# A weight-split step given a higher scheduling priority in a hybrid diffusion trunk kernel

## The chip, the cores and the metric

The kernel runs on one core of a Trainium2 chip. The metric is the device time of one execution in microseconds (us). Each core has five engines that run their own instruction lists in order and wait for one another through semaphores: TensorE (PE, matrix products; its weight loads are listed as PEld), VectorE (DVE), ScalarE (ACT), GpSimd (POOL) and SyncE (SP, which here only issues transfers).

## The reference

One step of a two-layer trunk on 128 context tokens and 256 latent tokens, D_MODEL = 1024, all in float32. Layer 0 mixes with a Mamba-2 head group and an RWKV-7 head group, layer 1 with a gated-linear-attention (GLA) and an mLSTM head group; each layer ends in a squared-ReLU MLP. Cut to its core:

```python
def sandwich_block(x, mod, mix_fn, g, w_up, w_down):
    shift1, scale1, gate1, shift2, scale2, gate2 = jnp.split(mod, N_MOD, axis=-1)
    m, st = mix_fn(rmsnorm(x, g[0]) * (1 + scale1) + shift1)
    x = x + gate1 * rmsnorm(m, g[1])
    f = jnp.square(jax.nn.relu((rmsnorm(x, g[2]) * (1 + scale2) + shift2) @ w_up)) @ w_down
    return x + gate2 * rmsnorm(f, g[3]), st

# mix_fn, layer 0: proj = h @ w_in (1024 x 6560); conv + SSD scan || RWKV-7 scan; concat @ w_out
# mix_fn, layer 1: proj = h @ w_in (1024 x 6192); GLA scan || conv + mLSTM; concat @ w_out
def rwkv step(s, inp):          # one of the scans
    s_kk = einsum('bhvk,bhk->bhv', s, kk_t)
    s = s * exp(lw_t) - s_kk[..., None] * (kk_t * a_t) + v_t[..., None] * k_t
    return s, einsum('bhvk,bhk->bhv', s, r_t)
```

The outputs are the two token arrays and the final scan states of each mixer.

## The kernel before

All 384 tokens stand side by side as the free dimension of [128, 384] tiles. The large products (input and output projections, MLP) are **dense** products. Their float32 operands are split in a high part, rounded to the matmul type, and a low part, the remainder: w = wH + wL and x = xH + xL, and each product is three matmuls, wH*xH, wH*xL and wL*xH. The activations are split once per layer. The weights come as panels, most of them 128 rows x 2 blocks x 128 columns (a 128x256 tile), 8 blocks in the MLP.

The way of a panel is: a transfer into a tile `raw` (line 695, from the SP queue), then `panel_split` (line 706): a copy on ScalarE, `wH<-raw` (line 714 through the helper on line 277), and a subtraction on VectorE, `wL<-raw,wH` (line 715 through line 235; a few go to GpSimd), then six matmuls `dps<-hnH,wH`, `dps<-hnL,wH`, `dps<-hnH,wL` for two blocks (lines 746 to 749 through line 221). `Dense.take(i)` (line 152) calls the split for the panel that it hands out and for `ahead` later ones, so that in source order a panel is split `ahead` panels before its matmuls. The buffers are few: in layer 0's mixer (line 1962) 5 raw tiles, 4 pairs of wH and wL, ahead 3; in layer 1's mixer 6, 6 and 4; in the MLP 3, 2 and 1. A wH copy therefore also waits until TensorE has read the panel that had the same buffer.

In the mixers the dense products are the filler of a pipeline. `run` (line 1584) draws steps from several generators (three stages of the RWKV-7 chain, `chain`, `inv` and `prep`; the SSD core; the dense panels as `fill`) by the pace table on line 34, and so sets the source order. That order is only a priority: the framework's scheduler walks a model of the engines, and on each engine it takes, of the instructions that are ready, the one that stands first in the source. What it puts out is the fixed list that each engine then runs on the chip. Tile names that come up below: `Zb`, `T`, `W`, `AO`, `pz`, `pt`, `pw`, `pe`, `pc` belong to the inverse of a 64x64 triangular matrix per head (`inv`), `R`, `UV`, `S`, `KR`, `py`, `pu`, `pd`, `pf` to the state chain, `psc`, `Q`, `BK` to its scores, and `cacc` is the accumulator of the 3x3 convolution.

The stages of the span: 0 to 60 us loads and the first norms, 60 to 170 us the start of layer 0's projections, 170 to 880 us layer 0's mixer with its end, 880 to 1185 us its MLP, 1185 to 1600 us layer 1's mixer, 1600 to 1851 us its MLP.

Of the kernel before, what the change touches and what calls it, by code (L numbers as in the profile page):

```python
# [8 lines left out]
F32 = mybir.dt.float32  # L9
# [5 lines left out]
ALU = mybir.AluOpType  # L15
# [160 lines left out]
class Net:  # L176
# [529 lines left out]
    def panel_split(self, cfg, raw):  # L706
        _, nk, ncol = raw.shape
        h = cfg["pool"].tile([128, nk, ncol], F32R, tag="wH", name="wH", bufs=cfg["split"])
        lo = cfg["pool"].tile([128, nk, ncol], F32R, tag="wL", name="wL", bufs=cfg["split"])
        hk = 512 // ncol  # L710
        self.nsplit += 1
        eng = self.nc.gpsimd if self.lpool and self.nsplit % self.lpool == 0 else None
        for q in (slice(i, min(nk, i + hk)) for i in range(0, nk, hk)):
            self.acopy(h[:, q], raw[:, q])
            self.tt(lo[:, q], raw[:, q], h[:, q].bitcast(F32), ALU.subtract, eng=eng)
        return h, lo

    def dacc(self):
# [1861 lines left out]
```

## Time and profile before

| | |
|---|---|
| median of 3 runs | 1855.35 us (1853.92 to 1860.46) |
| the profiled execution | 1853.32 us, its span 1851.2 us, 2.1 us outside the span |
| TensorE busy | 95% of the span, 13661 matmul records |
| TensorE weight loads | 80% |
| VectorE, ScalarE, GpSimd busy | 70%, 58%, 12% |
| mean granted clock of TensorE | 0.98 |
| chain that ended last | PE 75%, DVE 10%, ACT 8%, DMA 4% |

A share of busy time is a mean over stages with different limits: by the 40 slices of the page TensorE is busy for 70 to 90% of the first three slices and over 90% in nearly all later ones, VectorE is busiest in the mixers. Matmul ends are modelled, so that two matmuls that overlap in the pipeline both count; the start times are what to go by. The idle time in front of an instruction and what ended it stand in square brackets in a timeline.

### The profile page before, as it was taken

To read this page: it belongs to the slowest core of one execution; us is meant where nothing else is said; L and a number is where in the kernel's file an instruction comes from. 1 tells how busy PE (TensorE), PEld (TensorE's weight loads), DVE (VectorE), ACT (ScalarE), POOL (GpSimd) and SP (SyncE) were. 2 spreads that over 40 slices of the span, in tenths; PEclk is the share of its full clock that TensorE was granted. 3 is DMA by queue.
4 is the path that set the end of the run, shared out by engine and by line. 5 is a ranking of instruction groups with operands and counts; after the bars stand their busy time and mean duration, and the time that the engine had idled before them with its cause. 6 is when DMAs were issued, how large, how long until landed. Compare 5 with 4: busy or idle time off the path is not lost.

```text
span 1851.2 us, 37384 instructions
## 1 busy us (share of the span) xinstructions
PE 1765.5 (95%) x13661; PEld 1480.9 (80%) x13661; DVE 1301.8 (70%) x2992; ACT 1069.6 (58%) x2688; POOL 216.6 (12%) x270
## 2 busy tenths in 40 slices
PE   7879999999999999999999999899999998999998
PEld 3667767766666677786999998889989897999887
DVE  3698788777878889758766334786786958766434
ACT  3567475746574777646655333777676756755322
POOL 3222111110112011101000000020211212000000
PEclk9889999999999999999999999999999998999999
DMA  8332443333334322345445643333333233344432
GB/s 280 112 88 65 123 133 97 106 87 112 102 105 126 101 65 81 100 119 175 117 124 171 177 146 101 102 91 102 102 94 92 74 108 106 115 125 126 150 134 80
DMA packets 314107, 213.55 MB, mean 115 GB/s; under 512 B 39648, under 2 KB 297494, under 8 KB 313924
## 3 DMA queue, kind: packets, MB, share of 16 engines
q1 hardware_dynamic: 308756, 208.35, 38.6%
q10 hardware_dynamic: 4816, 2.69, 0.5%
q8 instruction: 107, 1.75, 0.4%
q14 instruction: 76, 0.62, 0.1%
q0 software_dynamic: 352, 0.13, 0.0%
HBM read 201.32 MB, written 9.78 MB: 114 GB/s over the span
## 4 chain that ended last, share of the span: by engine, by line
PE 75%; DVE 10%; ACT 8%; DMA 4%; issue 2%; POOL 1%; SPq 0%; DVEq 0%; ACTq 0%; POOLq 0%
PE dps L221 45%; PE o L221 7%; PE ps L221 4%; PE mod L221 3%; PE aux L221 2%; DVE wL L235 2%; PE psc L221 2%; DMA raw<-in_w_mod 2%; PE py L221 1%; PE pt L221 1%; DVE cacc L242 1%; PE pr L221 1%; ACT wH L277 1%; PE pw L221 1%; ACT Zb L277 1%
## 5 line engine op out<-in xcount | busy, mean ns | idle before, releaser
L277 ACT ACTIVATE wH<-raw 128x256 fp32r<-128x256 f32 (+1 forms) x790 | 363.3, 480 | 429.3 <-PE dps L221 309.6
L235 DVE TENSOR_TENSOR wL<-raw,wH 128x256 fp32r<-128x256 f32 (+2 forms) x771 | 398.9, 536 | 243.2 <-ACT wH L277 239.5
L277 ACT ACTIVATE Zb<-pz 64x384 f16<-64x384 f32 x160 | 77.2, 483 | 36.4 <-PE pz L221 34.1
L242 DVE SCALAR_TENSOR_TENSOR cacc<-rows,params,cacc 128x384 f32<-128x384 f32 (+1 forms) x192 | 94.2, 491 | 0.7
L221 PE MATMUL dps<-sH,wH 128*128 128x384 f32 x232 | 85.8, 371 | 4.0 <-DVE m L235 3.5
L221 PE MATMUL dps<-sL,wH 128*128 128x384 f32 x232 | 80.5, 347 | 0.3 <-DVE sL L235 0.2
L221 PE MATMUL dps<-sH,wL 128*128 128x384 f32 x232 | 79.7, 345 | 0.5 <-DVE wL L235 0.5
L221 PE MATMUL dps<-h0H,wH 128*128 128x384 f32 (+1 forms) x147 | 58.9, 401 | 8.2 <-ACT h0H L277 3.5
L235 DVE TENSOR_TENSOR AO<-AHb,rwmask 128x768 f16<-128x768 f16 (+1 forms) x112 | 60.1, 537 | 7.7 <-PE pz L221 6.0
L235 POOL TENSOR_TENSOR BK<-BK,kkk 128x768 f32<-128x768 f32 x16 | 33.8, 2110 | 221.5 <-DVE BK L239 150.5
L221 PE MATMUL mod<-xT,cond 128*32 128x384 f32 (+1 forms) x320 | 55.2, 485 | 3.8 <-DVE Q L235 2.5
L221 PE MATMUL dps<-h6H,wH 128*128 128x384 f32 (+2 forms) x147 | 54.9, 373 | 2.7 <-ACT wH L277 2.7
L221 PE MATMUL dps<-h2H,wH 128*128 128x384 f32 (+1 forms) x147 | 55.6, 378 | 1.4 <-ACT wH L277 1.4
L221 PE MATMUL dps<-h4H,wH 128*128 128x384 f32 (+1 forms) x147 | 54.9, 378 | 2.1 <-ACT h4H L245 2.1
L235 POOL TENSOR_TENSOR gDb<-gb 128x384 f32<-128x384 f32 x28 | 33.2, 1187 | 173.5 <-DVE gb L2230 73.2
L221 PE MATMUL dps<-h1H,wH 128*128 128x384 f32 (+1 forms) x147 | 52.0, 354 | 0.0
L221 PE MATMUL dps<-h6H,wL 128*128 128x384 f32 (+2 forms) x147 | 50.8, 346 | 1.2 <-DVE wL L235 1.2
L221 PE MATMUL dps<-h0H,wL 128*128 128x384 f32 (+1 forms) x147 | 51.7, 351 | 0.0
L221 PE MATMUL dps<-h1H,wL 128*128 128x384 f32 (+1 forms) x147 | 51.6, 351 | 0.0
L221 PE MATMUL dps<-h0L,wH 128*128 128x384 f32 (+1 forms) x147 | 51.5, 356 | 0.0
L221 PE MATMUL dps<-h1L,wH 128*128 128x384 f32 (+1 forms) x147 | 51.3, 355 | 0.0
L221 PE MATMUL dps<-h2H,wL 128*128 128x384 f32 (+1 forms) x147 | 51.1, 348 | 0.0
(1163 smaller groups left out, 5450.0 us busy)
## 6 DMA issues: line engine op xcount, KB each, us to landing
raw<-in_w_mlp_up SPq DMA_DIRECT2D x64, 512.0 KB
raw<-in_w_mlp_down SPq DMA_DIRECT2D x64, 512.0 KB
raw<-in_w_in_ab SPq DMA_DIRECT2D x204, 128.0 KB
xT<-in_w_mod SPq DMA_DIRECT2D x128, 192.0 KB
raw<-in_w_in_cd SPq DMA_DIRECT2D x192, 128.0 KB
raw<-in_w_mod SPq DMA_DIRECT2D x64, 192.0 KB
raw<-in_w_mod SPq DMA_DIRECT2D x32, 256.0 KB
raw<-in_w_out_cd SPq DMA_DIRECT2D x64, 128.0 KB
```

Of the source, the lines that this page charges most:

```text
L221: self.nc.tensor.matmul(out, lhsT, rhs, start=start, stop=stop)
L235: return (eng or self.nc.vector).tensor_tensor(out=out, in0=a, in1=b, op=op)
L242: self.nc.vector.scalar_tensor_tensor(out=out, in0=a, scalar=s, in1=b, op0=op0, op1=op1)
L277: self.nc.scalar.activation(out=out, in_=in_, func=AF.Copy)
```

## The change

The copy and the subtraction of `panel_split` are put in a block that lowers their priority number by 200, so that the scheduler ranks them as if they stood 200 instructions further up in the source. What they read, write and wait for stays as it is; no other priority changes. The number of instructions that compute is the same on every engine (2687 activations, 2992 on VectorE, 11552 matmul instructions); only their order moves.

```diff
         eng = self.nc.gpsimd if self.lpool and self.nsplit % self.lpool == 0 else None
-        for q in (slice(i, min(nk, i + hk)) for i in range(0, nk, hk)):
-            self.acopy(h[:, q], raw[:, q])
-            self.tt(lo[:, q], raw[:, q], h[:, q].bitcast(F32), ALU.subtract, eng=eng)
+
+        with self.tc.high_priority(offset=200):
+            for q in (slice(i, min(nk, i + hk)) for i in range(0, nk, hk)):
+                self.acopy(h[:, q], raw[:, q])
+                self.tt(lo[:, q], raw[:, q], h[:, q].bitcast(F32), ALU.subtract, eng=eng)
         return h, lo
```

Set side by side by instruction, the two orders differ so. Of the 176 subtractions on VectorE that ran between 170 and 800 us before, 133 now stand ahead of at least one instruction that they stood behind, 1342 such passings in all; of the 182 copies on ScalarE in that stretch it is 85, with 484 passings. Between 1185 and 1500 us it is 102 of 202 and 67 of 198; in the two MLPs (880 to 1185 and 1600 to 1851 us) 20 of 260 on VectorE. On TensorE the dense matmuls stand further ahead of the other matmuls in some places, by up to 22 near 275 to 330 us, 24 near 650 us, 16 near 790 us and 25 near 1480 us, and at the end of each such stretch the two orders meet again.

One place in layer 0's mixer, 284 to 297 us of the trace before, shows it on three engines. First VectorE, before: the subtractions of the panels 4231, 4267 and 4306 (the numbers tell the tiles apart).

```order
L235 TENSOR_TENSOR Q_4136<-psc_4168,rwmask_758 128x384
L235 TENSOR_TENSOR wL_4185<-raw_4182,wH_4184 128x256
L1382 COPY S_4210<-S0_2223 128x64
L1196 SCALAR_TENSOR_TENSOR b_4226<-r64_759,xT6_3651 128x384
L235 TENSOR_TENSOR R_4213<-pr_4212,R0_3523 128x64
L235 TENSOR_TENSOR wL_4231<-raw_4228,wH_4230 128x256
L235 TENSOR_TENSOR wL_4267<-raw_4264,wH_4266 128x256
L235 TENSOR_TENSOR xT6_3651<-b_4226,xT6_3651 128x384
L239 TENSOR_SCALAR UV_2678<-pu_4257 64x2x64
L235 TENSOR_TENSOR wL_4306<-raw_4303,wH_4305 128x256
```

And VectorE now: the same three subtractions, with the convolution taps (`cacc`) and, one row below this piece, `T_4047<-T_3975,pt2_4034`.

```order
L235 TENSOR_TENSOR wL_4231<-raw_4228,wH_4230 128x256
L242 SCALAR_TENSOR_TENSOR cacc_3929<-rows0_725,params_79,cacc_3929 128x384
L239 TENSOR_SCALAR UV_2678<-pu_4003 64x64
L242 SCALAR_TENSOR_TENSOR cacc_3929<-rows0_725,params_79,cacc_3929 128x384
L235 TENSOR_TENSOR wL_4267<-raw_4264,wH_4266 128x256
L242 SCALAR_TENSOR_TENSOR cacc_3929<-rows0_725,params_79,cacc_3929 128x192
L235 TENSOR_TENSOR modsb_3601<-modsb_3601,mod_4013 128x384
L242 SCALAR_TENSOR_TENSOR cacc_3929<-rows0_725,params_79,cacc_3929 128x192
L235 TENSOR_TENSOR W_4048<-W_3976,pw2_4027 128x384
L242 SCALAR_TENSOR_TENSOR cacc_3929<-rows0_725,params_79,cacc_3929 128x192
L235 TENSOR_TENSOR wL_4306<-raw_4303,wH_4305 128x256
L242 SCALAR_TENSOR_TENSOR cacc_3929<-rows0_725,params_79,cacc_3929 128x192
```

Before, `T_4047` stood 25 rows and more ahead of these subtractions; now all three stand ahead of it.

ScalarE at the same place, before: the copies `wH`, the chain's `Zb` and `UV`, the convolution's activation `Y`.

```order
L277 ACTIVATE wH_4230<-raw_4228 128x256
L277 ACTIVATE Zb_797<-pz_3994 64x6x64 x2
L245 ACTIVATE UV_2678<-pu_4003 64x64
L277 ACTIVATE wH_4266<-raw_4264 128x256
L277 ACTIVATE wH_4305<-raw_4303 128x256
L277 ACTIVATE Zb_797<-pz_4068 64x6x64 x2
L245 ACTIVATE Y_4008<-cacc_3929 128x384
L245 ACTIVATE Y_4008<-Y_4008 128x384 x2
L277 ACTIVATE W_4134<-pt_4119 128x384
L277 ACTIVATE xt_4280<-aux_4277 128x256
L245 ACTIVATE UV_2678<-pu_4147 64x64
```

ScalarE now: the copy of panel 4380, which stood behind `Z_4341<-dps_4181` further down, and the evacuation `Z_4341` of the dense column 4181 have come in front of `Zb_797<-pz_4068`.

```order
L277 ACTIVATE wH_4230<-raw_4228 128x256
L277 ACTIVATE Zb_797<-pz_3994 64x6x64 x2
L277 ACTIVATE wH_4266<-raw_4264 128x256
L245 ACTIVATE UV_2678<-pu_4003 64x64
L277 ACTIVATE wH_4305<-raw_4303 128x256
L277 ACTIVATE wH_4380<-raw_4378 128x256
L277 ACTIVATE Z_4341<-dps_4181 128x384
L245 ACTIVATE sg_4343<-Z_4341 128x384
L245 ACTIVATE sg_4343<-sg_4343 128x384
L277 ACTIVATE Zb_797<-pz_4068 64x6x64 x2
L245 ACTIVATE Y_4008<-cacc_3929 128x384
L277 ACTIVATE wH_4413<-raw_4411 128x256
```

`Zb_797<-pz_4068` now stands behind one more copy, an evacuation and two activations.

TensorE at the same place, before: the dense column `dps_4181` breaks off behind the second matmul of panel 4184, and the chain's `pz_4068` follows.

```order
L221 MATMUL dps_4181<-h5H_610,wH_3898 128x384
L221 MATMUL dps_4181<-h5L_611,wH_3898 128x384
L221 MATMUL dps_4181<-h5H_610,wL_3899 128x384
L232 MATMUL aux_4277<-const_base_77,X_3874 128x128
L221 MATMUL dps_4181<-h6H_619,wH_4184 128x384
L221 MATMUL dps_4181<-h6L_620,wH_4184 128x384
L221 LDWEIGHTS AO0_793
L221 MATMUL pz_4068<-T_4047,AO0_793 128x64
```

TensorE now: the column `dps_4181` is finished and the next one, `dps_4377`, begun ahead of `pz_4068`.

```order
L221 MATMUL dps_4181<-h6H_619,wH_4184 128x384
L221 MATMUL dps_4181<-h6L_620,wH_4184 128x384
L221 MATMUL dps_4181<-h6H_619,wL_4185 128x384
L221 MATMUL dps_4181<-h7H_628,wH_4184 128x384
L221 MATMUL dps_4181<-h7L_629,wH_4184 128x384
L221 MATMUL dps_4181<-h7H_628,wL_4185 128x384
L221 MATMUL dps_4377<-h0H_392,wH_4230 128x384
L221 MATMUL dps_4377<-h0L_393,wH_4230 128x384
L221 LDWEIGHTS AO0_793
L221 MATMUL pz_4068<-T_4047,AO0_793 128x64
```

Six dense matmuls have come in front of `pz_4068` here, and more stand between the chain's matmuls that follow.

## Rows read from the trace of the kernel before

**Rows 1.** The page, part 1: busy us, share of the span, instructions.

```profile
PE 1765.5 (95%) x13661; PEld 1480.9 (80%) x13661; DVE 1301.8 (70%) x2992; ACT 1069.6 (58%) x2688; POOL 216.6 (12%) x270
```

**Rows 2.** Stretches: length; PE, PEld, DVE, ACT, POOL busy us (count); clock, DMA share, GB/s.

```profile
60.00:170.00 110.00, 95.40 (x725) 78.40 (x724) 89.92 (x212) 73.97 (x191) 29.46 (x33) 0.88 0.33 89
170.00:800.00 630.00, 609.80 (x6879) 442.56 (x6877) 514.01 (x1283) 393.98 (x1009) 90.35 (x96) 0.99 0.36 102
...
880.00:1185.00 305.00, 299.25 (x1724) 287.67 (x1723) 170.06 (x351) 145.70 (x314) 9.46 (x22) 1.00 0.47 134
1185.00:1550.00 365.00, 351.12 (x2146) 329.70 (x2145) 279.59 (x636) 254.32 (x736) 55.03 (x70) 0.99 0.37 101
...
1600.00:1851.00 251.00, 244.88 (x1221) 222.09 (x1220) 131.65 (x249) 106.32 (x214) 0.00 (x0) 0.99 0.40 128
```

**Rows 3.** Stretch 170 to 800, instructions of wH: PE, PEld, DVE, ACT, POOL.

```profile
170.00:800.00 630.00, 216.48 (x726) 123.81 (x726) 81.77 (x176) 74.54 (x182) 3.77 (x5) 0.99 0.36 102
```

**Rows 4.** Waits of PE, 170 to 800: us in total, times, longest.

```profile
PE pw L221 <- ACT Zb L277: 3.1, 5, 1.3
PE pz L221 <- DVE T L235: 3.0, 5, 0.9
...
PE pd L221 <- ACT UV L245: 0.2, 1, 0.2
```

**Rows 5.** Waits of DVE and ACT for splits, 170 to 800.

```profile
DVE wL L235 <- ACT wH L277: 20.6, 35, 1.6
...
ACT wH L277 <- PE dps L221: 92.7, 81, 7.2
```

**Rows 6.** Waits of PE for splits, 60 to 170.

```profile
PE dps L221 <- ACT wH L277: 2.7, 1, 2.7
...
PE dps L221 <- DVE wL L235: 1.2, 1, 1.2
```

**Rows 7.** Timeline: start, us, instruction; first and last of the short handovers, 170 to 800.

```profile
174.79 0.29 DVE L235 TENSOR_TENSOR S<-Stmp,EBL 128x128 f32<-128x128 f32 x1
175.30 0.27 PE L232 MATMUL pf<-const_base,S 128*64 128x128 f32 x1
...
795.64 0.48 ACT L277 ACTIVATE Zb<-pz 64x384 f16<-64x384 f32 x1
796.24 0.35 PE L221 MATMUL pw<-W,Zb 128*128 128x64 f16 x6
```

**Rows 8.** Timeline of DVE at the place shown above.

```profile
284.56 0.55 DVE L235 TENSOR_TENSOR T<-T,pt 128x384 f16<-128x384 f16 x1
...
293.94 0.41 DVE L235 TENSOR_TENSOR wL<-raw,wH 128x256 fp32r<-128x256 f32 x1
...
295.35 0.75 DVE L235 TENSOR_TENSOR wL<-raw,wH 128x256 fp32r<-128x256 f32 x2
```

**Rows 9.** Timeline of PE at the same place.

```profile
286.21 0.34 PE L221 MATMUL dps<-h6L,wH 128*128 128x384 f32 x1
286.39 0.35 PE L221 MATMUL pz<-T,AO 128*128 128x64 f16 x6
287.37 0.19 PE L221 MATMUL pt<-Zb,W 64*64 64x64 f16 x1 [0.63 <-ACT Zb L277]
287.88 0.35 PE L221 MATMUL pt<-Zb,W 64*64 64x64 f16 x11 [0.32 <-ACT Zb L277]
...
288.55 0.93 PE L221 MATMUL psc<-KR,BK 64*128 64x128 f32 x6 [0.18 <-DVE BK L235]
...
295.34 0.44 PE L221 MATMUL dps<-h6H,wL 128*128 128x384 f32 x1
```

**Rows 10.** Timeline of ACT at the same place.

```profile
285.95 0.42 ACT L277 ACTIVATE wH<-raw 128x256 fp32r<-128x256 f32 x1 [1.97 <-PE dps L221]
286.84 0.99 ACT L277 ACTIVATE Zb<-pz 64x384 f16<-64x384 f32 x2 [0.47 <-PE pz L221]
```

## The prediction

> **What bounds the kernel now.** I read the shares of the engines first: TensorE is busy 95% of the span, the next engine 70% [rows 1]. Then the table by stretch, to see where TensorE is not busy. In the two MLPs it idles 305 - 299.25 = 5.8 us and 251 - 244.88 = 6.1 us, and layer 0's mixer from 170 to 800 us leaves 630 - 609.80 = 20.2 us, the start of the projections 110 - 95.40 = 14.6 us, layer 1's mixer 365 - 351.12 = 13.9 us [rows 2]. So no order of the splits can win more than a few ten us, and a win has to come out of these idle pieces.
>
> Next I asked what ends those pieces. In layer 0's mixer the 21 kinds of waits of TensorE that the view lists are for tiles of the chain (`Zb`, `T`, and so on, from 3.1 us in 5 waits down to 0.2 us in one), and none is for `wH` or `wL` [rows 4]: the split panels are there when TensorE comes to them. At the start of the projections two waits are for a split, 2.7 and 1.2 us [rows 6]. The other side of the splits is what they hold up. ScalarE stood 92.7 us in 81 waits in front of a `wH` copy whose buffer TensorE had not yet released, 1.14 us each, and VectorE 20.6 us in 35 waits in front of a `wL` whose `wH` was not there [rows 5]. Whatever stands behind them in the list stands too.
>
> Then the place from 284 to 297 us. VectorE works through convolution taps and chain steps, and a `wL` comes at 293.94 us, two more at 295.35 us [rows 8]. TensorE starts a dense matmul at 286.21 us and the next dense one only at 295.34 us, the first that needs the `wL` of 293.94 us; between them it does chain matmuls alone and idles 0.63 + 0.32 + 0.18 = 1.13 us on `Zb` and `BK` [rows 9]. So at a few places a split that is late on VectorE does cost something, though TensorE's wait is booked on the chain.
>
> **The change part by part.** Nothing is added or taken away; two kinds of instructions move. Each has a price and a gain.
>
> (a) The subtractions in layer 0's mixer: 133 of 176 move ahead of something, 1342 passings. What is passed starts one subtraction later if VectorE works without a break there: the pair at 295.35 us takes 0.75 us where one takes 0.41 [rows 8], so one more costs 0.33 us. TensorE feels it only where the passed result is wanted at once. From the timeline I counted, for matmuls between 170 and 800 us that are not dense, how long after their last input from another engine they start: 518 such handovers, 88 (17%) within 0.25 us, 196 (38%) within 0.8 us; the first of the 88 is `S` to `pf`, finished at 175.08 and read at 175.30 us, the last `Zb` to `pw`, 796.12 and 796.24 us [rows 7]. If one moved subtraction in six hits such a handover, that is 133 x 0.17 x 0.33 us = 7.5 us. Floor: 0, if dense matmuls cover every hit.
>
> (b) The copies on ScalarE: 85 of 182 move, a copy is 74.54 / 182 = 0.41 us [rows 3], so 85 x 0.17 x 0.41 us = 5.9 us, floor again 0, as long as the copy's buffer is free when ScalarE gets to it. If it is not, the price is the wait, which is the first rival.
>
> (a) and (b) together are 0 to 13.4 us. Dense matmuls have moved forward with the splits (eight stand ahead of `pz_4068` where two of them stood), so there is more cover than before; I take the middle, 6.7 us.
>
> (c) The gain in layer 0's mixer. Three stretches have a dense lead of more than 10 matmuls (near 275 to 330, 650 and 790 us). If each fills what the measured one shows, that is 3 x 1.13 us = 3.4 us; at most all the idle time of the stage, 20.2 us [rows 2]; at least 0, if TensorE waits for the same chain result after the dense matmuls instead of before them.
>
> (d) The start of the projections: the waits of 2.7 and 1.2 us [rows 6]. The copy behind the first of them passes a single instruction and stays behind evacuations that wait themselves, so I take half, 2.0 us, of at most 3.9.
>
> (e) Layer 1's mixer: 102 of 202 subtractions move. With the same share and price the loss is 102 x 0.17 x 0.33 us = 5.7 us, and the gain at most the 13.9 us of idle time. One long dense lead (near 1480 us) stands against it; I take 0, with ends of -5 and +6 us.
>
> (f) The MLPs: 20 of 260 subtractions move, TensorE idles under 2.5% [rows 2], its matmuls are the path: 0. Transfers: a raw tile is released a little earlier where its split moves up, and the DMA engines are 33 to 47% busy [rows 2], so 0.
>
> (g) Queues: SP issues the same transfers; GpSimd's own list of splits is almost unmoved, but its steps that read ScalarE's or VectorE's results share in (a) and (b).
>
> Sum: +6.7 - 3.4 - 2.0 + 0 = +1.3 us. The profiled execution took 1853.32 us, so the changed kernel's would take 1854.6 us; the median of the runs shown lies 2.0 us above that execution, so 1856.6 us, rounded 1857 us.
>
> TensorE counts as busy 97% of 170 to 800 us, while its weight loads fill 442.56 / 630 = 70% [rows 2]. The Trainium skill's page "Perfetto Trace Analysis" (section "Identifying the Most-Contended Engine") says that the matmul busy share is no good measure of how near TensorE is to its limit, and that the share of weight loads is a better one. By that rule the bound of gain (c) would not be 20.2 us but up to 30% of the stage, 187 us. The rows don't settle it, since many of these matmuls are longer than their weight loads; the sum stands on the 20.2 us.
>
> **The rivals.**
>
> Blocked lists (slower). A `wH` copy further up in ScalarE's list meets a buffer that TensorE still reads, and everything behind it stands. For it: this already happens in 81 of 182 cases [rows 5], a copy stood 1.97 us with the chain's `Zb` behind it [rows 10], and `Z_4341`, which waits for a whole dense column, now stands ahead of `Zb_797<-pz_4068`. Against it: where a copy moves up, the matmuls that free its buffer have often moved up too. Price: 85 moved copies x 81/182 x 1.14 us = 43 us of standing, of which 38% (the handovers within 0.8 us) reaches TensorE, 16 us: 1857 + 16 = 1873 us. It decides once ScalarE's standing before `wH` in that stage passes some 115 us.
> That ScalarE keeps strictly to its list is also what the Trainium skill's "Perfetto Trace Analysis" states (section "Tensor Engine Instruction (MATMUL, LD_WEIGHTS)"), and the wait in [rows 10] agrees.
>
> Filled droughts (faster). Dense work that is ready earlier fills the idle time while the chain runs, in more places than three, and the chain loses nothing because VectorE gets to the same point at the end of each backlog. For it: the 9 us without a dense matmul in [rows 9]. Against it: in [rows 4] the waits are for chain results, and these don't come earlier. Price: half of the 20.2 us, the 3.9 us of [rows 6] and 2 us of layer 1's mixer, 16 us: 1855 - 16 = 1839 us.
>
> Nothing to gain or lose. The splits have slack on both sides and the time stays at 1855 us. For it: no wait for a split in [rows 4]. Against it: 1342 passings on an engine that is busy 514.01 of 630 us [rows 2] are many.
>
> **How the numbers follow.** The forecast (1857 us) has 0.38, blocked lists 0.26, filled droughts 0.26, nothing 0.10. About 0.5% (9 us, so 1846 to 1864.6 us) is what a measurement of this kernel can tell from no change. The forecast's own range is 1855 + (0 - 9) to 1855 + (13 + 1), 1846 to 1869 us, from the floors and tops of (a) to (e); of its 0.38, 0.31 lies inside the bound, 0.05 above and 0.02 below. Nothing adds 0.10 inside. Blocked lists give 0.24 above and 0.02 inside, filled droughts 0.25 below and 0.01 inside. So faster 0.27, same 0.44, slower 0.29. The range reaches into both outer cases until a tenth is left at each end: 1838 to 1874 us.
>
> **What would show it.** In the changed profile: (a) and (b) right, if the waits of TensorE for `Zb`, `T`, `UV` and the like between 170 and 800 us grow by some 5 us; wrong, if that list stays at its sum. (c) right, if a dense matmul starts between `pz` and `psc` at the place shown and the idle time there shrinks below 1 us. (d) right, if the waits for `wH` and `wL` before 170 us come to about 2 us. Blocked lists are shown by ScalarE's 92.7 us growing past 115 us with the stage getting longer. The MLP stages must keep their lengths within 1 us. What would make the prediction wrong as a whole is a stage of layer 0's mixer that changes by over 10 us either way: then the order of the chain's steps against one another, of which I priced only the handovers to TensorE, is the larger effect.

## The result and the profile after

The changed kernel takes 1874.1 us (median of 4 runs, 1871.9 to 1874.6) against 1854.6 us for the kernel before (4 runs, 1851.6 to 1860.5): a ratio of 1.0106, with a 95% interval of 1.0087 to 1.0124. It is slower by 19.5 us where 2 us had been forecast. That is 5 us above the forecast's own range (1846 to 1869 us) and 0.1 us above the outer one (1838 to 1874 us). The profiled execution took 1874.24 us, its span 1872.0 us, 20.8 us more than before. The mean granted clock is 0.98 in both.

The page's first part, beside [rows 1]: all five engines have the same instructions, and TensorE counts as busy 7.7 us longer with the same 13661 matmuls.

```profile
PE 1773.2 (95%) x13661; PEld 1480.7 (79%) x13661; DVE 1311.8 (70%) x2992; ACT 1076.5 (58%) x2688; POOL 212.3 (11%) x270
```

To see where the time went I matched the two traces instruction by instruction and cut both at the same seven chain matmuls, chosen where equally many dense matmuls lie behind TensorE in both orders, so that each stretch holds the same dense work; up to eight of the other matmuls stand on the other side of a cut. The table by stretch of the kernel before (columns as in [rows 2]):

```profile
99.57:169.39 69.82, 60.08 (x546) 49.08 (x542) 59.51 (x135) 46.59 (x115) 16.71 (x17) 0.90 0.25 63
169.39:274.18 104.79, 102.52 (x1131) 74.09 (x1131) 84.22 (x214) 65.09 (x173) 17.35 (x15) 1.00 0.43 123
274.18:335.89 61.71, 60.10 (x751) 43.78 (x750) 53.62 (x137) 36.78 (x91) 6.51 (x7) 1.00 0.36 101
335.89:592.07 256.18, 245.13 (x2697) 174.29 (x2696) 202.34 (x502) 155.58 (x405) 37.52 (x34) 0.97 0.37 104
592.07:618.06 25.99, 25.30 (x254) 14.44 (x253) 19.42 (x53) 15.69 (x37) 2.53 (x2) 1.00 0.45 133
618.06:801.21 183.15, 178.57 (x2079) 137.43 (x2078) 155.62 (x385) 121.64 (x306) 26.44 (x38) 1.00 0.31 87
```

and the same stretches of the changed kernel:

```profile
95.93:171.41 75.48, 62.05 (x538) 49.25 (x534) 61.12 (x137) 47.69 (x117) 15.85 (x17) 0.91 0.27 68
171.41:276.19 104.78, 101.51 (x1139) 73.73 (x1139) 85.20 (x217) 66.38 (x176) 14.87 (x14) 1.00 0.43 122
276.19:344.06 67.87, 64.50 (x751) 44.62 (x750) 53.84 (x134) 36.77 (x92) 8.54 (x8) 0.97 0.32 90
344.06:599.32 255.26, 245.69 (x2697) 174.63 (x2696) 204.69 (x503) 156.77 (x404) 35.58 (x35) 0.98 0.37 104
599.32:630.06 30.74, 29.10 (x255) 16.11 (x254) 20.90 (x53) 14.86 (x35) 2.16 (x2) 0.83 0.36 107
630.06:822.46 192.40, 183.02 (x2078) 138.58 (x2077) 157.71 (x384) 123.03 (x308) 25.52 (x38) 0.99 0.30 86
```

Layer 0's mixer (the last five rows) grows by 19.2 us, and three stretches hold all of it: the first place, 274 to 336 us, +6.16 us; 592 to 618 us, +4.75; and the stretch from 618 us, with the second place in it, +9.25 (7.6 of it before 676 us). The other two give -0.01 and -0.92. The start ends 2.0 us later than before; in the MLPs and over layer 1's mixer as a whole the lag stays near 20.8 us.

Three things make up the 19.2 us. TensorE's idle time (length less busy time, summed) goes from 20.2 to 27.2 us: +7.0. Low clock (one minus the clock, times the length) goes from 256.18 x 0.03 = 7.7 to 2.0 + 5.1 + 5.2 + 1.9 = 14.2 us: +6.5 (the clocks are rounded to 0.01, so this is good to about 1 us). The remaining 5.7 us lie inside what the profile counts as busy. Over the whole execution the mean clock is the same: there TensorE idles 13.1 us more (1872.0 - 1773.2 = 98.8 against 1851.2 - 1765.5 = 85.7) and counts as busy 7.7 us more, and the low clock that layer 0's mixer has more is missing elsewhere. In layer 1's mixer, cut in the same way (1178.79 to 1565.10 us before, 1199.74 to 1586.79 us now), low clock goes from some 8 to 1 us, idle time grows by 3.8 us, and the length by 0.7 us.

At the first place TensorE's order is what the prediction had read from it. The timeline there, beside [rows 9]:

```profile
291.37 0.44 PE L221 MATMUL dps<-h0H,wH 128*128 128x384 f32 x1 [0.84 <-ACT Z L277]
...
291.82 0.35 PE L221 MATMUL pz<-T,AO 128*128 128x64 f16 x6
292.01 0.42 PE L221 MATMUL dps<-h0H,wL 128*128 128x384 f32 x1
...
295.17 0.49 PE L221 MATMUL psc<-KR,BK 64*128 64x128 f32 x2
...
308.70 0.45 PE L221 MATMUL pr<-S,KR 64*64 64x64 f32 x8 [0.60 <-DVE S L235]
310.57 0.38 PE L221 MATMUL pt<-i64h,W 64*64 64x64 f16 x12 [1.42 <-DVE W L235]
```

Dense matmuls now run between `pz` and `psc`, and nothing is idle there. But from `pz` to `psc` it now takes 3.35 us where [rows 9] has 2.16, and `pz` itself comes 5.43 us later than before: 2.0 us of that come from the start, the rest arises here, behind six more dense matmuls, one of which waited for a ScalarE result (`Z`). When the lead is used up, the chain stands alone at 308 to 311 us, with 0.60 + 1.42 us of idle time that the kernel before did not have. TensorE's idle time was not filled; there is more of it (3.37 us against 1.61), and it stands further back.

VectorE shows what these two waits stand behind. It works without a break up to `S` and `W`, and ahead of both comes a `KR` that takes 2.18 us where it took 0.55, while GpSimd's `BK` runs. First the kernel before, then the changed one:

```profile
301.56 0.55 DVE L235 TENSOR_TENSOR KR<-r,eI 128x384 f32<-128x384 f32 x1
...
301.72 2.07 POOL L235 TENSOR_TENSOR BK<-BK,kkk 128x768 f32<-128x768 f32 x1 [0.89 <-DVE BK L239]
```

```profile
305.57 0.43 DVE L235 TENSOR_TENSOR wL<-raw,wH 128x256 fp32r<-128x256 f32 x1
...
305.61 2.07 POOL L235 TENSOR_TENSOR BK<-BK,kkk 128x768 f32<-128x768 f32 x1 [2.42 <-PE dps L221]
...
305.91 2.18 DVE L235 TENSOR_TENSOR KR<-r,eI 128x384 f32<-128x384 f32 x1
```

A `wL` now stands directly in front of `KR`, and `KR` starts 0.30 us behind `BK` where it started 0.16 us ahead of it. So the two waits stand behind a collision of VectorE and GpSimd of 1.63 us, and not behind the dense work alone; no run takes it away by itself.

Waits for splits (first two views: ScalarE and VectorE, 170 to 820 us, beside [rows 5]; then TensorE, 60 to 170 us, beside [rows 6]):

```profile
ACT wH L277 <- PE dps L221: 104.0, 86, 8.1
```

```profile
DVE wL L235 <- ACT wH L277: 36.5, 63, 2.5
```

```profile
PE ps L232 <- DVE ssdt L235: 5.1, 1, 5.1
...
PE dps L221 <- ACT wH L277: 1.1, 1, 1.1
...
PE dps L221 <- DVE wL L235: 0.3, 1, 0.3
```

And TensorE's waits from 170 to 820 us, beside [rows 4]:

```profile
PE mod L221 <- DVE Q L235: 3.9, 3, 1.6
PE pw L221 <- ACT Zb L277: 3.4, 5, 1.1
...
PE pt L221 <- DVE W L235: 1.4, 1, 1.4
...
PE pz L221 <- DVE T L235: 1.0, 2, 0.5
```

### The profile page after: what moved, and what is told of

It reads as the page before. It is cut to its first block, busy times and chain, and to the rows that moved or that the text cites. A ratio compares the mean times of both kernels' runs of the same rounds, so it can differ in the third digit from the quotient of the medians.

```text
span 1872.0 us, 37461 instructions
## 1 busy us (share of the span) xinstructions
PE 1773.2 (95%) x13661; PEld 1480.7 (79%) x13661; DVE 1311.8 (70%) x2992; ACT 1076.5 (58%) x2688; POOL 212.3 (11%) x270
## 4 chain that ended last, share of the span: by engine, by line
PE 49%; DVE 4%; issue 1%; ACT 1%; DMA 1%; POOL 0%; DVEq 0%; SPq 0%; ACTq 0%; POOLq 0%
PE dps L221 35%; PE o L221 7%; PE ps L221 4%; DVE wL L235 1%; PE ms L221 1%; DVE acc L235 1%; PE mod L221 1%; PE ps L232 0%; DVE gE L235 0%; ACT wH L277 0%; PE warm L221 0%; DMA raw<-in_w_mlp_down 0%; DVE m L235 0%; POOL gDb L235 0%; DMA raw<-in_w_mod 0%
## 5 line engine op out<-in xcount | busy, mean ns | idle before, releaser
L235 DVE TENSOR_TENSOR wL<-raw,wH 128x256 fp32r<-128x256 f32 (+2 forms) x771 | 394.4, 529 | 285.9 <-ACT wH L277 264.4
L221 PE MATMUL dps<-h3H,wH 128*128 128x384 f32 (+1 forms) x147 | 51.7, 352 | 0.0
L221 PE MATMUL dps<-h3H,wL 128*128 128x384 f32 (+1 forms) x147 | 51.4, 350 | 0.0
L221 PE MATMUL dps<-h5H,wH 128*128 128x384 f32 (+1 forms) x147 | 51.4, 349 | 0.0
```

The costliest lines, as they stand in the source:

```text
L221: self.nc.tensor.matmul(out, lhsT, rhs, start=start, stop=stop)
L235: return (eng or self.nc.vector).tensor_tensor(out=out, in0=a, in1=b, op=op)
```

## The experiments

This table has, for every kernel that was run, the lengths in us of the three stretches between the same matmuls, in its profiled execution, and the medians. "Before" is the kernel before on the same chip in the same group of runs. The ratio is estimated from all executions of both kernels and isn't the quotient of the two medians.

| run | first place | 592 to 618 | 618 to 801 | median (runs) | before (runs) | ratio, 95% interval | low clock, rest |
|---|---|---|---|---|---|---|---|
| before | 61.71 | 25.99 | 183.15 | 1854.6 (4) | | | |
| after | 67.87 | 30.74 | 192.40 | 1874.1 (4) | 1854.6 (4) | 1.0106, 1.0087 to 1.0124 | -4, +23 |
| 1 | 67.98 | 30.40 | 190.11 | 1869.3 (8) | 1852.5 (13) | 1.0088, 1.0063 to 1.0114 | +9, +7 |
| 2 | 68.98 | 26.72 | 194.03 | 1873.4 (6) | 1852.5 (13) | 1.0104, 1.0071 to 1.0137 | +8, +11 |
| 3 | 71.80 | 29.92 | 198.61 | 1904.0 (4) | 1852.5 (13) | 1.0264, 1.0219 to 1.0309 | +25, +26 |
| 4 | 82.04 | 26.30 | 206.31 | 1893.0 (4) | 1852.5 (13) | 1.0222, 1.0192 to 1.0252 | +20, +21 |
| 5 | 61.79 | 25.51 | 182.13 | 1853.9 (10) | 1854.0 (19) | 1.0002, 0.9981 to 1.0023 | +2, -1 |
| 6 | 68.03 | 26.15 | 193.23 | 1871.9 (4) | 1854.0 (19) | 1.0087, 1.0059 to 1.0115 | -7, +24 |
| 7 | 65.24 | 29.01 | 198.23 | 1879.2 (4) | 1854.0 (19) | 1.0125, 1.0079 to 1.0171 | +5, +20 |
| 8 | 61.76 | 30.41 | 184.85 | 1851.6 (10) | 1854.0 (19) | 0.9989, 0.9972 to 1.0007 | +1, -2 |
| 9 | 67.62 | 31.52 | 183.74 | 1864.9 (10) | 1854.8 (29) | 1.0043, 1.0024 to 1.0061 | +7, +2 |
| 10 | 66.78 | 26.60 | 193.88 | 1871.0 (4) | 1854.8 (29) | 1.0078, 1.0056 to 1.0099 | +4, +11 |
| 11 | 61.52 | 25.87 | 184.86 | 1860.9 (10) | 1854.8 (29) | 1.0023, 1.0006 to 1.0040 | -8, +12 |
| 12 | 72.62 | 25.83 | 185.25 | 1849.4 (12) | 1854.8 (29) | 0.9973, 0.9950 to 0.9996 | -3, -2 |
| 13 | 73.27 | 25.65 | 182.56 | 1853.3 (11) | 1855.3 (23) | 0.9992, 0.9980 to 1.0005 | -1, 0 |
| 14 | 61.76 | 25.81 | 182.15 | 1848.2 (12) | 1855.3 (23) | 0.9966, 0.9943 to 0.9988 | -5, -1 |

The last column splits the mean difference from the kernel before, in whole us. For every execution the span and the mean granted clock are on record; one minus the clock, times the span, is its low clock, about what that can have cost, and the rest is its time without it. The kernel before has 36 to 40 us of low clock and a rest of 1815 to 1816 us in each of its four groups (84 executions, with whose mean the changed kernel is compared); the changed kernel has 36 us of low clock and a rest of 1838 us. So over the whole execution none of its loss is low clock.

**1 and 2: the priority at the two places alone, and everywhere else.**

```diff
-        with self.tc.high_priority(offset=200):
+        hi = self.nsplit - 1
+        with self.tc.high_priority(offset=200) if 90 <= hi < 112 or 184 <= hi < 206 else ExitStack():
```

> Only 44 of the 662 panels are hoisted, those of the two places in layer 0's mixer (near 285 to 320 and 630 to 665 us) where dense matmuls move up by 17 to 25. Order theory (dense matmuls in front of the chain's matmuls, the chain later without filler): the lag of the changed kernel grew by 6 us at the first place and 8 us at the second, so 1854.6 + 14 = 1869 us. Handover theory (each hoisted copy or subtraction delays what it passes, everywhere): 43 of 133 moved subtractions and 29 of 85 copies of this mixer, a third of its 18 us, 1861 us. Chance theory (the loss comes from clock drops that fall where they fall): any value between 1855 and 1875, with the low-clock time of the stage going with it.

> All panels are hoisted except those 44. Order theory: 1874.1 - 14 = 1860 us; what is left is the clock drop near 602 us (5 us) if it comes again. Handover theory: two thirds of the loss stay, 1868 us.

The first agrees with the order theory, 1869.3 us and the two places as long as in the changed kernel. But the second lost as much again, so the times don't add. By the last column the rests nearly do, 7 and 11 of 23 us; the other 9 and 8 us are low clock, so the first run's agreement in time is in good part luck. At the first place the second run has TensorE's order of the kernel before, but for two dense matmuls that stand a little further back, and still takes 68.98 us. Its table by stretch there:

```profile
285.00:290.00 5.00, 4.21 (x59) 3.45 (x57) 4.56 (x8) 1.80 (x4) 2.29 (x1) 1.00 0.26 87
290.00:295.00 5.00, 3.62 (x44) 2.96 (x45) 4.46 (x13) 2.34 (x5) 0.29 (x1) 0.89 0.12 40
295.00:300.00 5.00, 5.00 (x60) 4.37 (x59) 3.28 (x8) 1.26 (x3) 0.32 (x1) 0.50 0.01 2
```

TensorE idles 0.79 + 1.38 us there, where [rows 9] has 1.13, and then the granted clock falls from 1.00 to 0.50 (2.4 to 1.2 GHz). Of the 7.27 us lost there, (1 - 0.90) x 68.98 = 6.9 us are low clock. So the same place loses some 6 to 7 us in two ways: by the changed order (dense matmuls in front of the chain, and `KR` beside `BK`), or, without it, by a low clock, here behind waits of the chain that are a little longer (1.0 us for `S`, which the kernel before doesn't have there). That the longer waits are what lowered the clock is not shown: in run 12 it falls without them. The order theory, as put for the second run, is refuted by the time.

**3 and 4: TensorE's order of one kernel with all else of the other.** A list of the order in which one kernel runs its matmuls is added as dependencies that wait for nothing (`info()` makes one; shortened here):

```diff
+    for s in steps:
+        at += int(s)
+        i = byname.get("I-%d" % at)
...
+        if last is not None:
+            tc.add_manual_dep(i, last.name, info(), reason="pin")
+        last = i
```

> All panels are hoisted, but TensorE's matmuls are held in the order of the kernel before by order-only dependencies; 114 of 176 subtractions in layer 0's mixer still pass 807 instructions. Order theory: the loss goes, 1853 to 1859 us. Handover theory: at least half of the loss stays, 1864 us or more.

> No panel is hoisted, but TensorE's matmuls are held in the order of the changed kernel. Order theory: most of the loss is there without the priority, 1868 to 1876 us, or more, since the splits are now late for that order. Handover theory: 1855 to 1860 us.

Both mixed kernels are worse than either original: 40 to 52 us above the kernel before and 19 to 30 us above the changed one, and 20 to 25 us of the former is low clock. Neither theory as I had put it holds. My reading, which no run tests, is that TensorE's list and the others' lists fit one another, since one scheduler made them together. From here on, but for the seventh run, I fixed the order of every engine.

**5: three holds that missed their places.** Every engine's order is that of the kernel before, with extra multiplications on VectorE.

```diff
+        for _ in HOLD_AT:
+            for _ in range(7):
+                net.ts(hold, hold, 1.0, ALU.mult)
...
-        HOLDS.append((HOLD_AT[0], names[0]))
+        HOLDS.append(("I-%d" % HOLD_AT[0], names[0]))
```

(The last two lines are the mend that the ninth run has.)

> All engines keep the order of the kernel before. VectorE gets seven extra multiplications by one on a scratch tile of 128x64 (about 1 us together) at three points: ahead of a chain step near 215 us, where dense matmuls are at hand; ahead of the step that makes S near 287 us, where TensorE has chain matmuls alone; and ahead of Q near 592 us, the step that came late in the changed kernel. Theory A (an idle microsecond costs more than itself, since the granted clock falls after it): nothing to 0.3 us at 215 us; at the other two TensorE idles 0.5 to 1 us more and then runs at a granted clock of 0.50 for 5 to 14 us, so that each costs 3 to 7 us; time 1859 to 1866 us against 1852.5. Theory B (a late step costs its lateness): 0 + 1 + 1 us, no new stretch of low clock at the two points, 1853 to 1855 us.

The names of the three points were not matched, so all 21 multiplications ran between 1 and 6 us, where they cost nothing. The run says nothing on the two theories, but it is a control: with every order fixed the time is the same (1.0002), and its first place differs from that of before by 0.08 us.

**6: one collision taken away.** In the changed kernel, GpSimd's `E` near 599 us is made to wait for VectorE's second `cacc` (shortened here; the order of every engine is held as it was).

```diff
+    tc.add_manual_dep(byname["I-9131"], "I-9143", sync, reason="after cacc")
```

> The changed kernel with every engine's order as it was, and one wait more: GpSimd's sum E near 599 us starts only when VectorE's second cacc of that place has ended, so the two don't run side by side. Theory A (clock): cacc x2 goes back from 2.16 us to about 1.3, Q comes 0.9 us earlier, TensorE's idle time of 592 to 618 us falls to 0.7 us, and the 10.2 us at a granted clock of 0.50 don't come: 5 us less between these points, 1869 us against 1874. Theory B (only the lateness): 0.9 us less, 1873 us. If E itself is then late for its reader, no gain.

The timelines of VectorE and GpSimd, then two rows of the table by stretch, for the changed kernel:

```profile
598.87 2.16 DVE L242 SCALAR_TENSOR_TENSOR cacc<-rows,params,cacc 128x384 f32<-128x384 f32 x2
```

```profile
599.18 1.43 POOL L235 TENSOR_TENSOR E<-E 128x512 f32<-128x512 f32 x1 [2.77 <-ACT E L245]
```

```profile
600.00:605.00 5.00, 3.45 (x26) 1.53 (x26) 4.17 (x9) 0.72 (x2) 0.61 (x1) 0.66 0.17 45
605.00:610.00 5.00, 5.00 (x25) 2.63 (x25) 2.33 (x8) 0.83 (x2) 0.80 (x1) 0.50 0.45 155
```

and with `E` held:

```profile
599.20 1.26 DVE L242 SCALAR_TENSOR_TENSOR cacc<-rows,params,cacc 128x384 f32<-128x384 f32 x2
```

```profile
600.63 1.27 POOL L235 TENSOR_TENSOR E<-E 128x512 f32<-128x512 f32 x1 [3.89 <-ACT Zb L277]
```

```profile
600.00:605.00 5.00, 4.18 (x46) 2.40 (x46) 4.24 (x12) 0.97 (x2) 1.27 (x1) 1.00 0.22 64
605.00:610.00 5.00, 5.00 (x17) 1.66 (x16) 2.89 (x10) 1.35 (x3) 0.87 (x1) 1.00 0.84 268
```

With `E` beside it the pair of `cacc` takes 0.90 us longer; with `E` held, `Q` follows 0.9 us sooner, TensorE idles 0.82 us instead of 1.55 between 600 and 605 us, and the clock stays at 1.00. The stretch takes 26.15 instead of 30.74 us: 4.6 us for 0.9 us of lateness, which is theory A, in this execution. The price isn't fixed, though. In the profiled executions of all runs the collision (a second `cacc` of 1.5 to 1.6 us instead of 0.6) came seven times. The clock fell behind it in five (the changed kernel, runs 1, 3, 7 and 8; 29.01 to 30.74 us) and stayed at 1.00 in two (runs 2 and 10; 26.72 and 26.60 us). In the eight without collision or hold it never fell (25.51 to 26.30 us). The median falls by 2 us only, which the intervals don't tell from no change; in the profiled execution 3.4 us of low clock came between 336 and 400 us, where the changed kernel had none. The Trainium skill's page "SBUF — State Buffer" (section "Summary: rules for kernel authors") says that a VectorE operation with two SBUF inputs and a GpSimd operation that reads SBUF can't run together, and the second to issue waits. The rows agree: `E` ends at 600.61 us and the second `cacc` 0.42 us after.

**7: the subtraction alone.**

```diff
             self.acopy(h[:, q], raw[:, q])
+            with self.tc.high_priority(offset=200):
                 self.tt(lo[:, q], raw[:, q], h[:, q].bitcast(F32), ALU.subtract, eng=eng)
```

> Only the subtraction has the priority, the copy stands at its own place. The lead of the dense matmuls at the two places (up to 17 and 23) is there as in the changed kernel. Theory L (the lead of the dense matmuls pushes the chain back): +4 to +7 us between 274 and 336 us and +5 to +8 between 618 and 676 us, 1865 to 1873 us in all. Theory C (ScalarE's lists are what costs): within 4 us of the kernel before, 1851 to 1856 us.

1879.2 us: with the copies at their old rank the loss is as large as with both (20 us of it in the rest), so moved copies aren't needed for it. The places take +3.5 us, at a clock of 1.00 and with a `KR` of 0.55 us, and +4.9 us (618 to 676 us, with 22 matmuls fewer in front of the cut), just under what the lead theory had said; 9.9 us more are lost from 676 to 730 us, with 8.3 us of low clock, which neither theory had.

**8: another order of the start.** Up to 274 us the order that the fourth run had, from there that of the kernel before.

> No priority. Up to 274 us every engine has the order that it had in the fourth experiment (TensorE's matmuls as in the changed kernel, the others fitted to it), and from there on that of the kernel before. In that experiment the matmuls at 270 us came 3.7 us earlier than before. If that is a gain that lasts: 1847 to 1850 us against 1852.5. If the rest gives it back (by a later stretch of low clock): 1852 to 1856 us.

The matmul at 274 us comes at 270.00 us instead of 274.18, as hoped, but between 592 and 618 us the run loses 4.4 us with the same instructions in the same order: `E` of the sixth run collides here too, with 5.2 us of low clock behind it. 1851.6 us, ratio 0.9989: not told from no change.

**9: the holds in place.**

> As the fifth experiment, but with the seven multiplications (195 ns each there) now standing where they were meant to: ahead of Stmp near 215 us, of Stmp near 287 us (it makes the S that TensorE reads) and of Q near 592 us; all else in the order of the kernel before. Theory A (idle time at a place without dense matmuls lowers the granted clock): at most 0.5 us at 215 us; at 287 and at 592 us some 1.4 us of lateness, of which TensorE idles about 1, and behind it 5 to 14 us at a granted clock of 0.50, so 3.5 to 8 us each; 1860 to 1868 us against 1854. Theory B (lateness only): 1 to 1.4 us at each of the two, 1856 to 1857 us.

The holds at the two later points on VectorE, and the table by stretch for both:

```profile
285.40 1.57 DVE L239 TENSOR_SCALAR hold<-hold 128x64 f32<-128x64 f32 x7
```

```profile
596.76 2.63 DVE L239 TENSOR_SCALAR hold<-hold 128x64 f32<-128x64 f32 x7
```

```profile
272.34:339.96 67.62, 64.52 (x751) 47.31 (x750) 55.16 (x144) 36.93 (x91) 6.52 (x7) 0.92 0.33 92
596.16:627.68 31.52, 28.36 (x254) 16.04 (x253) 21.76 (x60) 15.70 (x37) 2.52 (x2) 0.84 0.37 109
```

The first hold, near 215 us, cost 0.5 us. The one at the first place took 1.57 us and cost 5.91 (67.62 - 61.71), with 67.62 x 0.08 = 5.4 us of low clock; the one at 592 us took 2.63 us and cost 5.53, with 5.0 us of low clock. Theory A by its numbers, in a kernel whose order is that of before; and over all ten executions 7 of the 8 us lost are low clock.

**10 and 11: the local order put in, and taken out.** In the tenth all engines have the order of the kernel before, but between 274 and 336 and between 618 and 676 us that of the changed one; the eleventh is the changed kernel with the order of before in these two stretches, and `E` held.

> Every engine keeps the order of the kernel before, except between 274 and 336 us and between 618 and 676 us: there all of them have the order of the changed kernel. If the local order of all engines is what costs there, +5 to +7 us in the first stretch and +6 to +9 in the second, and 1866 to 1870 us. If the loss needs what was changed earlier (phase of GpSimd and transfers), under +3 us in each, 1854 to 1860 us.

> The opposite: every engine has the order of the changed kernel, except in the two stretches, where all have that of the kernel before; and GpSimd's E near 599 us waits for cacc as in the sixth experiment. If these three spots are the whole loss: the lag behind the kernel before stays under 4 us all through layer 0's mixer, 1855 to 1858 us. If the losses come back elsewhere: 1865 to 1874 us.

The tenth's table by stretch at the first place and from 618 us:

```profile
273.36:340.14 66.78, 62.93 (x751) 43.66 (x750) 54.46 (x137) 36.76 (x91) 6.21 (x7) 1.00 0.34 93
...
619.51:813.39 193.88, 184.35 (x2079) 140.21 (x2076) 157.98 (x385) 122.45 (x306) 25.40 (x38) 0.98 0.29 82
```

+5.07 us at the first place, at a clock of 1.00 throughout: 2.2 us more idle time (3.85 against 1.61) and 2.8 us more busy time for the same 751 matmuls. So the local order of all engines costs 5 us without any low clock; the collision of `KR` is in it (2.19 us here too). In the second stretch +10.7 us, 7.4 of them before 676 us, with some 2 us of low clock. Taken out, the three stretches of the eleventh are those of before to 0.2, 0.1 and 1.7 us, and the median falls by 13 of the 19.5 us, with `E` held as well. By the last column the order of the two places is worth 11 us of rest put in, and 12 of the 23 us of rest are still there when it is taken out: the two places are about half of the loss. What is left by time (6.2 us) is lost elsewhere in its profiled execution: 7.2 us between 100 and 169 us, 5.3 between 336 and 400 with 4.8 us of low clock, and 3.9 us gained near 530.

**12: the start's order and `E` held.**

> The eighth experiment with GpSimd's E near 592 us held until cacc has ended. There the matmuls at 274 us came 2.3 us earlier than before, and 4.4 us were lost between 592 and 618 us with 5.2 us of clock. If holding E takes that loss away as in the sixth: 1846 to 1849 us against 1854. If other stretches of low clock take its place: 1850 to 1854 us.

1849.4 us, ratio 0.9973 (0.9950 to 0.9996): just faster than before. 592 to 618 us is back at 25.83 us. But its profiled execution took 1861.2 us, since the first place lost 10.9 us. Up to there it has the order of the eighth run on every engine. The twelfth, then the eighth, by stretches of 5 us:

```profile
280.00:285.00 5.00, 3.86 (x42) 3.27 (x42) 4.72 (x15) 2.96 (x6) 0.00 (x0) 0.98 0.04 13
285.00:290.00 5.00, 5.00 (x53) 4.09 (x51) 3.07 (x7) 1.00 (x3) 0.61 (x1) 0.50 0.13 43
```

```profile
280.00:285.00 5.00, 3.87 (x49) 3.30 (x48) 5.00 (x16) 2.59 (x6) 0.00 (x0) 1.00 0.15 50
285.00:290.00 5.00, 5.00 (x90) 4.18 (x90) 4.40 (x11) 1.88 (x5) 0.61 (x1) 1.00 0.13 43
```

Equal order, equal idle time (1.14 and 1.13 us), and the clock falls in one and not in the other. The place stands on an edge, which by itself can part two executions by 11 us; those of the kernel before lie between 1849 and 1863 us.

**13 and 14: the first place filled.** Four dense matmuls that stood ahead of `pz_4068` move behind it, into its two waits for `Zb`; on the order of before, and on the twelfth. In instruction numbers:

```diff
-    4274 4275 4309 4310  4074(pz) 4087(pt) 4088(pt)
+    4074(pz) 4274 4275 4309  4087(pt) 4310 4088(pt)
```

> The order of the kernel before on every engine, but for four matmuls of TensorE at the first place: the dense ones on h5 and h6 that stood ahead of pz_4068 now stand behind it, three before the first matmul on Zb and one after it, where TensorE idled 0.63 and 0.32 us. Theory A (those idle pieces are what lets the granted clock fall there in some executions): the idle time of 285 to 290 us falls from 1.13 us to under 0.5, the clock there stays at 1.00, and besides the 0.5 us that the chain gains the executions with 13 us of low clock at this place disappear: median 1849 to 1853 us against 1854.8. Theory B (the clock falls there for another reason): 1854 us, spread as before.

> The twelfth experiment (the order of the fourth up to 274 us, then that of the kernel before, E held) with the same four matmuls moved. Theory A: the loss of 10.9 us between 274 and 336 us of the twelfth's profiled execution is gone, 1842 to 1847 us, and the slowest execution comes below 1858 us. Theory B: 1848 to 1850 us, as in the twelfth.

The thirteenth can't decide between the theories, since the edit did not do what it was to do: TensorE still idles 0.92 us from 285 to 290 us (and 0.45 before), over the whole place 1.77 us where it was 1.61. The clock falls, and the place takes 73.27 us. The median, 1853.3 us, is not told from no change. The fourteenth had no low clock there in its profiled execution and takes 1848.2 us, ratio 0.9966 (0.9943 to 0.9988), the fastest of all, but its slowest execution is 1862.4 us, so the edge may still be there. The fourteenth beats both kernels; that it owes anything to the four matmuls is not shown, since the twelfth is as fast within its interval.

## Why the prediction was wrong

The step that failed is (c), the dense lead, which I priced as a gain of 1.13 us in each of three stretches, with no gain as its worst case. Where it was to gain, the changed order costs: 5.1 us at the first place and 7.4 at the second, shown by putting the local order into the kernel before (run 10), and gone when it is taken out of the changed one (run 11). The third stretch (730 to 801 us) grew by 0.9 us. The two places are about half of the loss, 11 of the 23 us at full clock.

The reading behind (c) was wrong in one place: I took the stretch without dense matmuls for one in which a lead can only gain. TensorE idled 1.13 of the 9 us; for the rest it worked on the chain, at full clock. Dense matmuls put ahead of the chain then can't fill more than the 1.13 us, and they push the chain back; what they had filled later is empty afterwards. The sum had no term for that. So I read the timelines; runs 10 and 11 exchange whole stretches, with the subtractions and copies that moved there, and don't part the lead from them. One piece belongs to the subtractions by the rows: the `KR` behind a moved `wL`, late by a few tenths of a microsecond, which then lost 1.63 us beside `BK`.

Both marks that I had set for (c) were met (a dense matmul between `pz` and `psc`, under 1 us of idle time) while the stretch grew by 6.16 us: I had asked of the spot, and should have asked of the stretch up to the point where the lead is back at zero.

The second failure is a term that the sum lacked. All through I took a late microsecond of TensorE to cost a microsecond. In single executions it cost more: 0.9 us of lateness between 592 and 618 us 4.6 us (run 6), and 1.57 us at the first place 5.9 (run 9), since the granted clock fell to half behind the idle time. It decides what a stretch takes, but not the 19.5 us, since the changed kernel has no more low clock as a whole. No row of the profile before shows that as a price, though its clock does fall: 0.97 between 336 and 592 us. What that cost can be read from run 10, which has the same order there: it takes 49.33 us at a clock of 1.00 for the stretch from 400 to 453 us, where the kernel before takes 53.70 us at 0.90.

The range, 1846 to 1869 us, doesn't come out of its own sum either: the floors and tops of (a) to (e) add up to -29 and +19 us, 1826 to 1874 us, and the measured time lies at that top.

The other steps:

- (a) and (b), handovers made late, 6.7 us: idle time in layer 0's mixer grew by 7.0 us, and TensorE's list of waits from 18.8 to 24.9 us in sum, which was the sign that I had set. But it did not come in the way priced, and the agreement is luck. Outside the three stretches nothing was lost (-0.9 us), and of the list only some waits grew (`Q` 2.5 to 3.9 us, `Zb` 3.1 to 3.4), while `T` fell from 3.0 to 1.0. The price of one passed instruction, spread evenly over 133 + 85 of them, has no support.
- (d), the start: the waits for splits fell from 3.9 to 1.4 us, 2.5 where I had 2.0. But the gain was lost again at once: `ps` waits 5.1 us for `ssdt` where it waited 1.3, and the stretch from 99.57 us is 5.7 us longer. Net +2.0 instead of -2.0.
- (e), layer 1's mixer, 0: right in the number, by another balance. The lag grows to 26 us and more in the middle of the stage and is back at 20.7 at its end; 3.8 us more of idle time stand against some 7 us less of low clock, of which no term spoke. (f), the MLPs, 0: right. The lag changes by 0.5 us at most there.
- "Blocked lists" gave 1873 us, which is nearly the time measured, but not by that mechanism: ScalarE's 92.7 us became 104.0, under the 115 us that were to decide it, and without any moved copy the loss is as large (run 7). "Filled droughts" and "nothing" are refuted by the time.
- The sign that I had named for "wrong as a whole", a stage of layer 0's mixer that changes by over 10 us, came true (+19.2). The cause named there was the order of the chain's steps against one another; what the runs show is the order of all the work of two places, the chain's and the dense.

What stays open: the other half of the loss, 12 us at full clock that run 11 still has. By the rows it lies at the start (5.7 us longer from 99.57 us, at nearly the same clock) and in layer 1's mixer (0.7 us longer with 7 us less of low clock); no run tests that. Then 5.7 us of the mixer's loss lie inside TensorE's busy time, and 2.8 us of the first place's at a clock of 1.00 in run 10. The single matmuls are not longer there; they overlap less, as the 32 `mod` matmuls of the place show, which take 498 ns each in both and cover 5.9 us before and 7.5 us in run 10 (instructions by group: busy us, mean ns, idle time before):

```profile
L221 PE MATMUL mod<-xT,cond 128*32 128x384 f32 x32 | 5.9, 498 | 0.0
```

```profile
L221 PE MATMUL mod<-xT,cond 128*32 128x384 f32 x32 | 7.5, 498 | 0.0
```

How much of that is the model of their ends, no run shows. Open too is what decides whether the clock falls at the first place in a given execution (runs 8 and 12).

## What to carry to other kernels

A stretch without dense matmuls is a drought only as far as TensorE idles in it; a priority that brings dense work forward there can delay the chain and leave the real gap further back. Where the granted clock falls to half after a short gap, price a late result by the gap and the low clock behind it, which came to two to five times the lateness here (2.63 us held cost 5.5, 0.9 us cost 4.6), in the executions in which it fell. Before two orders are compared by time, split each time into low clock and rest: runs 1 and 2 read otherwise then. When an order made by a scheduler is in question, exchange whole stretches, with all engines: one engine's list in the other's surroundings was worse than both.

## What the runs showed of the hardware that was not expected

- The granted clock fell to 0.50 behind idle pieces of 0.63, 0.32 and 0.18 us among short chain matmuls (run 12), and stayed at 1.00 behind the same pieces in another run (8). With every order fixed, a stretch without low clock mostly repeats to some 0.2 us (the first place takes 61.71, 61.79, 61.76 and 61.76 us in the kernel before and in runs 5, 8 and 14; the stretch from 730 us, with 70.15 to 71.80 us, is the exception); the low clock is what differs.
- A GpSimd `E` and a VectorE `cacc` that overlap cost the later one the wait: 2.16 instead of 1.26 us for `cacc` x2 in the changed kernel, while in the kernel before `cacc` came first and `E` took 1.66 us instead of 1.27. A shift of some tenths of a microsecond chose which (`E` starts 592.22 - 592.07 = 0.15 us behind the cut before, and 599.32 - 599.18 = 0.14 us ahead of it in the changed kernel). At the first place the same lies between `KR` (0.55 or 2.18 us) and `BK`.
